# Up-projection of a decoder trunk: seven half-size products per pair in place of eight, and the output projection in column halves

## The chip, the core and the metric

The kernel runs on one core of a Trainium2 chip. The metric is the device time of one execution in microseconds (us); lower is better. The core's engines work through their own instruction streams in order: TensorE (PE) for matrix products, VectorE (DVE), ScalarE (ACT), GpSimd (POOL), and SyncE (SP), whose queue issues all the transfers named here. An instruction starts when those ahead of it on its engine are through and the semaphores that it waits for have been raised.

## What is computed

One layer of a decoder: three token mixers, their gated sum `merged`, and then the part that the change touches (S = D = 1024, D_FF = 2816):

```python
x = x + merged @ w_o[l]
x = x + _conv_ffn(_rmsnorm(x, norm_ffn[l]), ffn_w_up[l], ffn_conv_w[l], ffn_conv_b[l], ffn_w_down[l])
...
def _conv_ffn(h, w_up, conv_w, conv_b, w_down):
    u = h @ w_up
    up = jnp.pad(u, ((0, 0), (CONV_WIDTH - 1, 0), (0, 0)))
    u = sum(conv_w[j] * up[:, j:j + S] for j in range(CONV_WIDTH)) + conv_b
    gate, val = jnp.split(u, 2, axis=-1)
    return (jax.nn.silu(gate) * val) @ w_down
```

## The kernel before

Every product is made in three: an operand is split into a rounded high part (`act`, on ACT) and the rest, its low part (`tt`, source minus high part, on DVE or POOL); `hilo` (L105) makes both. Then high x high, high x low and low x high are summed in one accumulation. A matmul takes 128 columns of weights and 512 of the moving operand.

Four stages matter here. `phase_a` ends with the branch products (tile `bps`) and loads and splits `w_o`. `phase_o` (L1289) takes eight blocks of 128 rows: it splits `merged` (`mh`, `ml`), multiplies by `w_o` in two column halves (`ops_`, 24 matmuls each), adds x, stores the sum to DRAM (`xD`), and calls `norm_block`: Square on ACT, the reciprocal root on POOL (`rs_r`), `y` on DVE, eight transposes on PE (`ntp`), and the split into `h2h` and `h2l`. `phase_up` makes the 2816 gate and 2816 value channels in 22 pairs of 128 + 128. For each of the two columns of a pair: 48 matmuls into a two-bank PSUM tile `ups_`, then the causal convolution of width 3 straight from PSUM (ACT `Identity` into `cv`, two `stt` on DVE); then Silu on ACT and the product with the value on POOL into `self.g`, which stays in SBUF. The weights are loaded and split a column ahead (`whi` on ACT, `wlo` on POOL). `phase_down` (L1358) multiplies g by `w_down`, 22 steps of 24 matmuls for each half of the rows; its first weights and its first g (`dn0`, `g0`) are made during `phase_up`.

No order is written out by hand: a list scheduler with its own cost table lays out every engine's stream when the program is built, and it is fixed from then on. Tile pools with a stated number of buffers decide what waits for what.

## Time and profile before

| | us |
|---|---|
| time, median of 3 runs | 2163.57 (2162.49 to 2165.92) |
| the profiled execution: time | 2172.32 |
| its span | 2170.5 |
| mean granted TensorE clock, share of full speed | 0.989 |
| first `ups_` matmul to first `dps_` matmul | 1438.06 to 1913.29 |

The span is one execution seen by the hardware profiler, 1.8 us short of that execution's own time. The profile gives the busy time of each engine, the idle time before an instruction, and what ended it. A matmul's shown length (0.39 us) overlaps the next; the distance from start to start is what one costs.

### The profile page before, as it was taken

How to read it: one execution, taken by the hardware profiler on the slowest of the kernel's cores; microseconds unless marked ns; L12 is line 12 of the kernel's file. 1: busy time of each engine (PE TensorE's matmuls, PEld its weight loads, DVE VectorE, ACT ScalarE, POOL GpSimd, SP SyncE). 2: the span in 40 equal slices, each digit the busy share in tenths (PEclk: the TensorE clock that was granted, in tenths of full speed). 3: DMA queues.
4: the chain of work that ended last, by engine and by line, in shares of the span. 5: the costliest groups of instructions: out<-in, count | busy, mean ns of one | idle time of the engine just before them, and what ended most of it. 6: DMA issues, size and time to landing. Idle time of an engine off the chain costs nothing. (4 is left out here: it accounts for less than half of the span.)

```text
span 2170.5 us, 32037 instructions
## 1 busy us (share of the span) xinstructions
PE 2098.8 (97%) x12818; PEld 1680.4 (77%) x12818; DVE 945.1 (44%) x1956; ACT 740.2 (34%) x1270; POOL 694.0 (32%) x522
## 2 busy tenths in 40 slices
PE   7999999999999998999888999999999999999998
PEld 6877777777777776777677777888888888878887
DVE  7035255243433523566677764432222222243534
ACT  5332222232232223666545442232222222232322
POOL 3152333152243323364155556013333333300000
PEclk9999999999999999999999999999999999999999
DMA  5222232122222214300375444221111111142521
GB/s 178 84 71 78 63 88 66 51 85 62 73 68 78 82 60 131 95 16 11 94 221 175 149 145 160 97 80 49 49 49 49 49 49 49 39 155 98 174 98 59
DMA packets 127447, 191.39 MB, mean 88 GB/s; under 512 B 60064, under 2 KB 64032, under 8 KB 127296
## 3 DMA queue, kind: packets, MB, share of 16 engines
...
q14 instruction: 50, 0.41, 0.1%
...
## 5 line engine op out<-in xcount | busy, mean ns | idle before, releaser
L89 POOL TENSOR_TENSOR wlo<-wraw,whi 128x512 fp32r<-128x512 f32 (+1 forms) x174 | 276.1, 1594 | 582.4 <-ACT whi L86 245.3
L65 PE MATMUL gps<-hhi,whi 128*128 128x512 f32 (+1 forms) x880 | 346.5, 397 | 8.1 <-ACT sp L86 5.4
L65 PE MATMUL gps<-hlo,whi 128*128 128x512 f32 (+1 forms) x880 | 342.6, 392 | 0.0
L86 ACT ACTIVATE whi<-wraw 128x512 fp32r<-128x512 f32 (+1 forms) x174 | 128.0, 737 | 426.4 <-DMA wraw<-in_w_rest_dram 106.3
L65 PE MATMUL gps<-hhi,wlo 128*128 128x512 f32 (+1 forms) x880 | 226.2, 394 | 2.1 <-DVE lx L99 1.7
L65 PEld LDWEIGHTS gps<-hhi,whi 128*128 128x128 f32 x880 | 168.0, 191 | 49.4 <-ACT sp L86 6.2
L65 PEld LDWEIGHTS gps<-hlo,whi 128*128 128x128 f32 x880 | 167.9, 191 | 36.0 <-issue 4.5
L65 PEld LDWEIGHTS gps<-hhi,wlo 128*128 128x128 f32 x880 | 157.4, 188 | 43.1 <-issue 6.7
L89 POOL TENSOR_TENSOR rs_r<-rs_v,phalf 128x1 f32<-128x1 f32 (+2 forms) x43 | 40.2, 935 | 391.9 <-DVE rs_v L96 383.8
L86 ACT ACTIVATE L<-L,m 128x128 f32<-128x128 f32 (+7 forms) x128 | 98.8, 772 | 69.1 <-DVE m L89 47.5
L77 PE MATMUL ptp<-ident,L 128*128 128x128 f32 x432 | 72.4, 282 | 10.7 <-DVE L L99 2.9
L89 DVE TENSOR_TENSOR gl<-g,gh 128x512 fp32r<-128x512 f32 x43 | 29.5, 692 | 108.8 <-ACT gh L86 107.6
L99 DVE SCALAR_TENSOR_TENSOR st<-pr,gam,fc 128x64 f32<-128x64 f32 x60 | 17.0, 283 | 128.0 <-PE pr L65 127.8
L86 ACT ACTIVATE gh<-g 128x512 fp32r<-128x512 f32 x43 | 26.8, 630 | 131.9 <-PE dps__19477 L65 67.2
L77 PEld LDWEIGHTS ptp<-ident,L 128*128 128x128 f32 x432 | 49.2, 142 | 26.9 <-issue 15.0
L89 POOL TENSOR_TENSOR g<-cv 128x1024 f32<-128x1024 f32 x22 | 52.6, 2390 | 51.7 <-DVE cv L99 50.2
L878 DVE CUSTOM_DVE_ANT_0 L<-S,mband,rq 128x512 f32<-128x512 f32 (+3 forms) x96 | 57.1, 612 | 19.5 <-PE ptp L77 9.7
L89 DVE TENSOR_TENSOR wdl<-wdr,wdh 128x1024 fp32r<-128x1024 f32 x44 | 53.8, 1225 | 15.9 <-ACT wdh L86 15.9
L86 ACT ACTIVATE sp<-gps,hbg 128x512 f32<-128x512 f32 x48 | 32.9, 686 | 75.1 <-PE gps L65 67.9
L65 PE MATMUL bps<-oh,whi 128*128 128x512 f32 x128 | 53.2, 421 | 5.1 <-DVE merged L99 3.2
L89 POOL TENSOR_TENSOR merged<-merged,gth 128x512 f32<-128x512 f32 x32 | 47.6, 1491 | 29.1 <-DVE gth L99 26.3
L878 DVE CUSTOM_DVE_ANT_0 L<-S,bias 128x512 f32<-128x512 f32 (+3 forms) x96 | 50.7, 551 | 12.5 <-PE ptp L77 6.1
...
## 6 DMA issues: line engine op xcount, KB each, us to landing
wraw<-in_w_up_dram SPq DMA_DIRECT2D x44, 512.0 KB, 3.3
wdr<-in_w_down_dram SPq DMA_DIRECT2D x44, 512.0 KB, 3.3
wraw<-in_w_rest_dram SPq DMA_DIRECT2D x80, 256.0 KB, 2.9
pD<-sp SPq DMA_DIRECT2D x78, 256.0 KB, 2.0
gth<-pD SPq DMA_DIRECT2D x48, 256.0 KB, 3.0
x<-in_x_dram SPq DMA_DIRECT2D x16, 512.0 KB, 5.5
wraw<-in_w_rw_dram SPq DMA_DIRECT2D x28, 256.0 KB, 3.0
draw<-pD SPq DMA_DIRECT2D x24, 256.0 KB, 5.0
```

What stands on the lines that cost most here:

```text
L65: ins = self.nc.tensor.matmul(out, lhsT, rhs, start=start, stop=stop)
L77: self.marked(self.nc.tensor.transpose(out, in_, ident))
L86: self.nc.scalar.activation(out, in_, func, **kw)
L89: (eng or self.nc.vector).tensor_tensor(out, a, b, op)
L99: self.nc.vector.scalar_tensor_tensor(out, a, s, b, op0, op1)
L878: self.nc.vector.tensor_tensor_reduce(L[:, c0:c0 + w], ps[:, :w], bias[:, c0:c0 + w], scale, 3.0e38, ALU.add, ALU.min, acc)
```

## The change

**Up-projection.** Rows 0 to 511 and 512 to 1023 of the normed input, each cut in two halves of the 1024 summed channels, and the gate and value weights, cut the same way, form a 2 x 2 by 2 x 2 product, which is made with seven half-size products (`n2`, `m4`, `m3`, `n5`, `m1`, `m6`, `m7`) in place of eight: 7 x 12 matmuls a pair in place of 96. The seven moving operands (`X`) are made once, in `operands`, while the norms run; the seven weights of a pair are made in `up_weight`, five of them from a sum or difference of two raw blocks (`wsum`, DVE), then a high part (`wh`, ACT) and a low part (`wl`, POOL; for `m6` DVE). The products come together from three banks in `after` into `C` in SBUF, and the convolution reads `C`.

**Output projection.** First all eight blocks for columns 0 to 511, then for columns 512 to 1023 in the order 0, 1, 4, 2, 5, 3, 6, 7, with norm, transposes and `operands`. The first half of `w_o` lies in a pool of its own (`woa`), whose memory takes `xm1` and `xm6`; that of `merged` takes `xm7` and raw up-weights.

**g** goes through DRAM (`gD`): stored by pair, read back in `phase_down` by `down_g`, in 44 loads; `dn0` and `g0` are gone.

```diff
+            self.W, self.woa = [], self.pool(woa, "woa", 1, "right")
+            for c, wp in enumerate((self.woa, self.pool(wob, "wob", 1, "right"))):
...
-    def phase_o(self):
+    def phase_o(self, wob, up):
...
+            seq = [(0, b) for b in range(8)] + [(1, b) for b in (0, 1, 4, 2, 5, 3, 6, 7)]
+            nxt = split(0)
+            for n, (c, b) in enumerate(seq):
+                mh, bs = nxt, slice(128 * b, 128 * b + 128)
+                if c and b == 0:
+                    for m, tag in (("m1", "woh"), ("m6", "wol")):
+                        t = self.woa.tile([128, 2, 4, 512], F32R, tag=tag, name="x" + m)
+                        self.X[m] = [t[:, 0], t[:, 1]]
                 x = xp.tile([128, D], F32, tag="x2", name="x2")
...
+                cs = slice(512 * c, 512 * c + 512)
+                if c:
+                    nc.sync.dma_start(x[:, 0:512], self.xD[b, :, 0:512])
+                nc.sync.dma_start(x[:, cs], self.i["x"][0, bs, cs])
+                ps = aps.tile([128, 512], F32, tag="o", name="ops_")
+                w = self.W[c]
+                self.mm3(ps, lambda k: (mh[0][:, k], mh[1][:, k]), lambda k: (w[0][:, k], w[1][:, k]), 8)
+                self.tt(x[:, cs], ps, x[:, cs], ALU.add)
+                if n < 15:
+                    nxt = split(seq[n + 1][1])
...
+                    self.up_open(wob, up)
+                    ts = rows()
+                    for m, k in (("n2", 0), ("m4", 4)):
+                        self.up_w[0, m] = self.up_weight(0, m, [t[:, k:k + 4] for t in ts])
+                    for m in ("n2", "m4"):
+                        self.up_begin(0, m)
+                nc.sync.dma_start(self.xD[b, :, cs], x[:, cs])
+                if not c:
+                    continue
+                y, p = self.norm_rows(x, g, o2, 1), []
+                for q in range(2):
+                    p.append(tps.tile([128, 4, 128], F32, tag="ntp", name="ntp"))
+                    for k in range(4):
+                        col = 128 * (4 * q + k)
+                        self.tr(p[q][:, k], y[:, col:col + 128], self.ident)
+                if b == 7:
+                    for j, m in ((1, "n2"), (1, "m4"), (0, "m3")):
+                        self.up_prepare(j, m)
+                self.operands(b, p, o2)
+            for m in ("n5", "m1", "m6", "m7"):
+                self.up_prepare(0, m)
...
+    def operands(self, b, p, sp):
...
+        lower, vec, pool = b < 4, self.nc.vector, self.nc.gpsimd
+        first, second, names = (p[0], p[1], ("n2", "m4")) if lower else (p[1], p[0], ("n5", "m3"))
+        bs = slice(128 * (b % 4), 128 * (b % 4) + 128)
+        T = lambda tag: sp.tile([128, 4, 128], F32, tag=tag, name=tag, bufs=1)
+        at = lambda n: [t[:, :, bs] for t in self.X[n]]
+        neg, dif, a = T("neg"), T("dif"), T("xa")
+        kept = [self.hD[b % 4, k].rearrange("p (k n) -> p k n", k=4) for k in range(3)]
+        self.act(neg, first, scale=-1.0)
+        self.tt(dif, second, neg, ALU.add)
+        self.hilo(*at(names[0]), neg)
+        self.hilo(*at(names[1]), dif, lo_eng=pool if lower else vec)
+        if lower:
+            self.act(a, second)
+            self.nc.sync.dma_start(kept[0], neg)
+            self.nc.sync.dma_start(kept[1], a)
+            return
+        c = T("xc")
+        self.nc.sync.dma_start(a, kept[0])
+        self.nc.sync.dma_start(c, kept[1])
+        self.tt(a, a, neg, ALU.add, pool)
+        h, l = at("m1")
+        self.act(h, a, scale=-1.0)
+        self.stt(l, a, -1.0, f32v(h), ALU.mult, ALU.subtract)
+        self.tt(dif, dif, a, ALU.subtract)
+        self.hilo(*at("m6"), dif, lo_eng=vec)
+        self.tt(c, c, neg, ALU.subtract, pool)
+        self.nc.sync.dma_start(kept[2], c)
...
+    def up_open(self, wob, up):
...
+        t = self.mgp.tile([128, 2, 4, 512], F32R, tag="mb", name="xm7")
+        self.X["m7"] = [t[:, 0], t[:, 1]]
+        t = self.mgp.tile([128, 3, 8, 128], F32, tag="ma", name="wraw")
+        self.raw.update({(1, 1): t[:, 0], (0, 0): t[:, 1], (1, 0): t[:, 2]})
+        for j, e in ((1, 1), (0, 0), (1, 0)):
+            self.up_load(j, e)
+        wob.close()
...
+    def up_weight(self, j, n, w=None):
+        a = lambda e, k: self.raw[j % 2, e][:, 4 * k:4 * k + 4]
+        x, y, op = {"n2": ((1, 0), (1, 1), ALU.add), "m4": ((1, 1), None, None), "m3": ((0, 0), None, None),
+                    "n5": ((0, 0), (0, 1), ALU.add), "m1": ((0, 0), (1, 1), ALU.add),
+                    "m6": ((1, 0), (0, 0), ALU.subtract), "m7": ((0, 1), (1, 1), ALU.subtract)}[n]
+        src = a(*x)
+        if y:
+            src = self.wsum[0]
+            self.wsum = self.wsum[1:] + self.wsum[:1]
+            self.tt(src, a(*x), a(*y), op)
+        vec = w or n == "m6"
+        w = w or [self.upr.tile([128, 4, 128], F32R, tag=n + m, name="w" + m) for m in "hl"]
+        self.hilo(*w, src, lo_eng=self.nc.vector if vec else None)
+        return w
...
+    def up_begin(self, j, n):
...
+        if n == "n2":
+            for m in "bc":
+                u[m] = self.ups.tile([128, 512], F32, tag=m, name="ups_" + m)
+        if n == "m1":
+            u["a"] = self.upq.tile([128, 512], F32, tag="a", name="ups_a")
+        ps = u[{"n2": "b", "m4": "c", "m3": "b", "n5": "c", "m1": "a", "m6": "b", "m7": "c"}[n]]
+        self.up_product(ps, n, self.up_w.pop((j, n)), n in ("n2", "m4", "m1"))
+        return ps
+    def up_product(self, ps, n, w, first):
+        x = self.X[n]
+        terms = [(k, a, c) for k in range(4) for a, c in ((0, 0), (0, 1))] + [(k, 1, 0) for k in range(4)]
+        for i, (k, a, c) in enumerate(terms):
+            self.mm(ps, w[a][:, k], x[c][:, k], first and i == 0, i == 11, skip_group_check=not first)
...
+            def after(j, n, ps):
+                u = self.pairs[j]
+                if n == "n2":
+                    u["C"] = [t2.tile([128, S], F32, tag="C%d" % e, name="C") for e in range(2)]
+                gate, val = u["C"]
+                if n in ("n2", "m4", "m1"):
+                    u[n] = T(n)
+                    self.act(u[n], ps)
+                if n == "m4":
+                    self.tt(val[:, lo], u["m4"], u["n2"], ALU.subtract, nc.gpsimd)
+                elif n == "m3":
+                    u["w"] = T("w")
+                    self.tt(u["w"], ps, val[:, lo], ALU.add)
+                elif n == "n5":
+                    self.stt(gate[:, hi], ps, -1.0, u["w"], ALU.mult, ALU.add)
+                elif n == "m6":
+                    self.tt(val[:, hi], ps, u["m1"], ALU.add)
+                elif n == "m7":
+                    self.tt(gate[:, lo], ps, u["m1"], ALU.add)
...
+            def conv(j, C):
...
+                for e in (1, 0):
+                    c, t = j + NFF * e, T("cv%d" % e, S)
+                    self.act(t, C[e], AF.Identity, scale=cw[:, c, 2:3], bias=cw[:, c, 3:4])
+                    for d in (1, 2):
+                        self.stt(t[:, d:], C[e][:, :S - d], cw[:, c, 2 - d:3 - d], t[:, d:], ALU.mult, ALU.add)
                     ts.append(t)
-                self.act(ts[0], ts[0], AF.Silu)
-                self.tt(self.g[:, j], ts[0], ts[1], ALU.mult, nc.gpsimd)
+                self.act(ts[1], ts[1], AF.Silu)
+                self.tt(ts[1], ts[1], ts[0], ALU.mult, nc.gpsimd)
+                nc.sync.dma_start(self.gD[j], ts[1])
...
+            start = [((1, "n2"), ""), ((1, "m4"), ""), ((0, "m3"), ""), ((0, "n5"), "1m3 1n5"), ((1, "m3"), ""),
+                     ((1, "n5"), ""), ((0, "m1"), ""), ((0, "m6"), "1m1"), ((0, "m7"), "1m6"), ((1, "m1"), "1m7 2n2"),
...
+            for j in range(2, NFF):
+                for n in self.ORDER:
+                    after(j, n, self.up_begin(j, n))
+                    self.up_prepare(last[0] + 1, last[1])
+                    last = j, n
+                    if n == "n5":
+                        loads(j + 2)
...
+    def down_g(self, pool, j, cols, bufs, tag="graw"):
+        raw = pool.tile([128, 512], F32, tag=tag, name="graw", bufs=bufs)
+        self.nc.sync.dma_start(raw, self.gD[j, :, cols])
...
-                        self.hilo(*g, self.g[:, j, tgs], lo_eng=nc.vector)
+                    w, g = self.down_w(wp, j), self.down_g(gp, j, tgs, 4)
                     ws.append((j, w, g))
```

**Where instructions stand now.** On DVE, in the middle of `phase_up` before, there was nothing but the convolution, each pair of rows reading the PSUM tile `ups_`:

```order
L99 SCALAR_TENSOR_TENSOR cv_16597<-ups__16596,cw_15988,cv_16597 128x1023
L99 SCALAR_TENSOR_TENSOR cv_16597<-ups__16596,cw_15988,cv_16597 128x1022
L99 SCALAR_TENSOR_TENSOR cv_16656<-ups__16655,cw_15988,cv_16656 128x1023
L99 SCALAR_TENSOR_TENSOR cv_16656<-ups__16655,cw_15988,cv_16656 128x1022
L99 SCALAR_TENSOR_TENSOR cv_16717<-ups__16716,cw_15988,cv_16717 128x1023
```

On DVE after, one whole pair (`w` and `C` with `ups_` are sums out of PSUM, `wsum` a sum of two raw weight blocks, named once where both lie in one tile, `cv1`/`cv0` the convolutions; the pair's other two rows, `w` and a first `C` out of PSUM, stand just ahead):

```order
L89 TENSOR_TENSOR wsum1_16122<-wraw_16113 128x512
L89 TENSOR_TENSOR wsum_15289<-wraw_15290 128x512
L89 TENSOR_TENSOR C_17705<-ups_b_17690,m1_17783 128x512
L89 TENSOR_TENSOR wl_17834<-wsum0_16121,wh_17833 128x512
L89 TENSOR_TENSOR wsum0_16121<-wraw_16113 128x512
L99 SCALAR_TENSOR_TENSOR cv1_17821<-C_17705,cw_16244,cv1_17821 128x1023
L89 TENSOR_TENSOR C_17704<-ups_c_17691,m1_17783 128x512
L99 SCALAR_TENSOR_TENSOR cv1_17821<-C_17705,cw_16244,cv1_17821 128x1022
L89 TENSOR_TENSOR wsum1_16122<-wraw_16113,wraw_15290 128x512
L89 TENSOR_TENSOR wsum_15289<-wraw_15290,wraw_16113 128x512
L99 SCALAR_TENSOR_TENSOR cv0_17825<-C_17704,cw_16244,cv0_17825 128x1023
L99 SCALAR_TENSOR_TENSOR cv0_17825<-C_17704,cw_16244,cv0_17825 128x1022
```

On POOL after, the same pair, from one `C` to the next (before, a pair was two `wlo` 128x1024 and one product `g`):

```order
L89 TENSOR_TENSOR C_17705<-m4_17725,n2_17706 128x512
L89 TENSOR_TENSOR cv0_17678<-cv0_17678,cv1_17674 128x1024
L89 TENSOR_TENSOR wl_17765<-wraw_16113,wh_17764 128x512
L89 TENSOR_TENSOR wl_17787<-wsum1_16122,wh_17786 128x512
L89 TENSOR_TENSOR wl_17805<-wsum_15289,wh_17804 128x512
L89 TENSOR_TENSOR wl_17857<-wsum1_16122,wh_17856 128x512
L89 TENSOR_TENSOR wl_17877<-wsum_15289,wh_17876 128x512
L89 TENSOR_TENSOR wl_17895<-wraw_15290,wh_17894 128x512
L89 TENSOR_TENSOR C_17852<-m4_17872,n2_17853 128x512
```

What moved: the convolution reads `C` in SBUF, six more instructions with both inputs in SBUF stand between its parts, and POOL has eight instructions a pair where it had three.

At the end of the output projection, on PE before, 24 matmuls of the first up-projection column stood ahead of the last block's transposes (their end is shown), and more of that column behind them:

```order
L65 MATMUL ups__15996<-h2h_15271,whi_15961 128x512
L65 MATMUL ups__15996<-h2l_15272,whi_15961 128x512
L65 MATMUL ups__15996<-h2h_15271,wlo_15962 128x512 x8
L77 MATMUL ntp_15943<-ident_93,y_15936 128x128 x4
L77 MATMUL ntp_15950<-ident_93,y_15936 128x128 x4
L65 MATMUL ups__15996<-h2h_15271,whi_15961 128x512
L65 MATMUL ups__15996<-h2l_15272,whi_15961 128x512
```

On PE after, around the sixth block's transposes (row block 3, `ntp_15987`), and then on ACT between the fifth block's `neg` and that block's `neg` (`y_15980` is the sixth block's Square):

```order
L77 MATMUL ntp_15913<-ident_95,y_15906 128x128 x4
L77 MATMUL ntp_15918<-ident_95,y_15906 128x128 x4
L65 MATMUL ops__16086<-woh1_14930,ml_16039 128x512 x3
L77 MATMUL ntp_15987<-ident_95,y_15980 128x128 x4
L77 MATMUL ntp_15992<-ident_95,y_15980 128x128 x4
L65 MATMUL ups_b_16130<-xn2h_15278,mh_16123 128x512
L65 MATMUL ups_b_16259<-xn2h_15278,wh_16176 128x512
```

```order
L86 ACTIVATE neg_15923<-ntp_15918 128x512
L86 ACTIVATE y_15980,ss_15979<-x2_15943 128x1024
L86 ACTIVATE wh_16180<-wraw_16113 128x512
L86 ACTIVATE xn5h_15284<-neg_15923 128x4x128
L86 ACTIVATE wh_16184<-wraw_16113 128x512
L86 ACTIVATE wh_16214<-wsum_15289 128x512
L86 ACTIVATE wh_16176<-wsum0_16121 128x512
L86 ACTIVATE xm1_15595<-xa_15925 128x4x128
L86 ACTIVATE xm3h_15282<-dif_15924 128x4x128
L86 ACTIVATE wh_16209<-wsum1_16122 128x512
L86 ACTIVATE neg_15997<-ntp_15987 128x512
```

What moved: three matmuls stand between the two sets of transposes, and the first up-projection matmul stands right behind; on ACT eight splits stand between the Square and the next `neg`.

On SP before, at the end of `phase_up`, the final norm's gain and the second to fourth down-weights (the first stands 43 rows earlier):

```order
L1366 DMA gf_18654<-in_norm_final_dram 128x1024
L1354 DMA wdr_18688<-in_w_down_dram 128x1024
L1354 DMA wdr_18722<-in_w_down_dram 128x1024
L1354 DMA wdr_18756<-in_w_down_dram 128x1024
L1378 DMA x3_19330<-xD_60 128x1024
```

On SP after, at the same place:

```order
L1536 DMA graw_19642<-gD_62 128x512
L1536 DMA graw_19678<-gD_62 128x512
L1536 DMA graw_19714<-gD_62 128x512
L1489 DMA gD_62<-cv0_19415 128x1024
L1548 DMA gf_19446<-in_norm_final_dram 128x1024
L1529 DMA wdr_19456<-in_w_down_dram 128x1024
L1529 DMA wdr_19492<-in_w_down_dram 128x1024
```

What moved: `gf` and the first down-weight `wdr` now stand behind the store of the last pair's g, and that store waits for POOL's last product.

## Rows read from the trace of the kernel before

**Rows 1.** The page: busy time of each engine, share of the span, instructions.

```profile
PE 2098.8 (97%) x12818; PEld 1680.4 (77%) x12818; DVE 945.1 (44%) x1956; ACT 740.2 (34%) x1270; POOL 694.0 (32%) x522
```

**Rows 2.** Windows: us, busy (count) by engine, granted clock, DMA share, GB/s.

```profile
1420.00:1438.00 18.00, 18.00 (x88) 14.97 (x87) 6.08 (x9) 3.33 (x6) 0.55 (x1) 1.00 0.14 56
1750.00:1850.00 100.00, 100.00 (x443) 82.84 (x442) 23.08 (x18) 25.73 (x23) 32.42 (x14) 1.00 0.14 48
2030.00:2130.00 100.00, 100.00 (x439) 82.12 (x439) 45.11 (x59) 33.64 (x52) 2.19 (x4) 1.00 0.41 137
```

**Rows 3.** Timeline of POOL, DVE and ACT in the up-projection, one pair: start, us, engine.

```profile
1701.43 2.41 POOL L89 TENSOR_TENSOR wlo<-wraw,whi 128x1024 fp32r<-128x1024 f32 x1 [8.47 <-ACT whi L86]
...
1716.22 1.06 ACT L86 ACTIVATE cv<-cv 128x1024 f32<-128x1024 f32 x1 [2.80 <-DVE cv L99]
...
1723.19 2.41 POOL L89 TENSOR_TENSOR wlo<-wraw,whi 128x1024 fp32r<-128x1024 f32 x1 [8.48 <-ACT whi L86]
1724.34 2.60 DVE L99 SCALAR_TENSOR_TENSOR cv<-ups__17495,cw,cv 128x1023 f32<-128x1023 f32 x2 [8.21 <-ACT cv L86]
1727.08 2.39 POOL L89 TENSOR_TENSOR g<-cv 128x1024 f32<-128x1024 f32 x1 [1.48 <-DVE cv L99]
```

**Rows 4.** The page's groups: busy, mean ns of one, idle before and releaser.

```profile
L89 DVE TENSOR_TENSOR gl<-g,gh 128x512 fp32r<-128x512 f32 x43 | 29.5, 692 | 108.8 <-ACT gh L86 107.6
L86 ACT ACTIVATE gh<-g 128x512 fp32r<-128x512 f32 x43 | 26.8, 630 | 131.9 <-PE dps__19477 L65 67.2
L89 POOL TENSOR_TENSOR g<-cv 128x1024 f32<-128x1024 f32 x22 | 52.6, 2390 | 51.7 <-DVE cv L99 50.2
```

**Rows 5.** Timeline of DVE and POOL at the end of `phase_a`.

```profile
1307.59 3.51 POOL L89 TENSOR_TENSOR merged<-merged,gth 128x512 f32<-128x512 f32 x2
1308.64 3.54 DVE L89 TENSOR_TENSOR wol<-woraw,woh 128x1024 fp32r<-128x1024 f32 x2 [2.48 <-ACT woh L86]
...
1323.33 1.22 DVE L89 TENSOR_TENSOR wol<-woraw,woh 128x1024 fp32r<-128x1024 f32 x1
1323.49 2.21 POOL L89 TENSOR_TENSOR merged<-merged,gth 128x512 f32<-128x512 f32 x1 [1.49 <-DVE gth L99]
...
1329.28 1.29 POOL L89 TENSOR_TENSOR merged<-merged,gth 128x512 f32<-128x512 f32 x1
```

**Rows 6.** Groups by form, 1343 to 1438 (output projection).

```profile
L99 DVE SCALAR_TENSOR_TENSOR y<-x,rs_r,gain 128x1024 f32<-128x1024 f32 x7 | 9.0, 1285 | 5.0 <-POOL rs_r L89 5.0
L86 ACT ACTIVATE h2h<-ntp 128x512 fp32r<-128x512 f32 x14 | 7.6, 596 | 50.5 <-PE ntp L77 50.5
L86 ACT ACTIVATE y<-x 128x1024 f32<-128x1024 f32 x7 | 7.4, 1062 | 10.5 <-issue 8.0 <-DVE x L89 2.5
L89 POOL TENSOR_TENSOR rs_r<-rs_v,phalf 128x1 f32<-128x1 f32 x7 | 3.9, 551 | 74.7 <-DVE rs_v L96 74.7
```

**Rows 7.** What PE waited for, 1300 to 2170: us in total, times, longest.

```profile
PE dps__18661 L65 <- DVE cv L99: 1.8, 1, 1.8
...
PE ups__15996 L65 <- ACT h2h L86: 0.2, 1, 0.2
PE ups__15996 L65 <- DVE h2l L89: 0.2, 1, 0.2
```

**Rows 8.** Timeline of PE where the up-projection ends.

```profile
1924.22 0.47 PE L65 MATMUL dps__18661<-wdh,g 128*128 128x512 f32 x1 [1.84 <-DVE cv L99]
...
1925.31 0.63 PE L65 MATMUL dps__18662<-wdh,g 128*128 128x512 f32 x1
1925.73 0.63 PE L65 MATMUL dps__18662<-wdl,g 128*128 128x512 f32 x1
```

**Rows 9.** Windows there (columns as in the second group).

```profile
1926.00:1928.00 2.00, 2.00 (x6) 1.54 (x6) 1.42 (x2) 2.00 (x4) 0.59 (x1) 0.50 0.98 344
1928.00:1930.00 2.00, 2.00 (x10) 1.64 (x9) 2.00 (x4) 1.90 (x4) 0.00 (x0) 1.00 1.00 387
```

**Rows 10.** Transfers: count, KB each, median us from issue to landing.

```profile
wdr<-in_w_down_dram SPq DMA_DIRECT2D x44, 512.0 KB, 3.3
...
gth<-pD SPq DMA_DIRECT2D x48, 256.0 KB, 3.0
...
xD<-x SPq DMA_DIRECT2D x8, 512.0 KB, 2.6
```

More of the change, by code (lines that the diff above doesn't have):

```diff
@@ L193, in norm_block, with norm_rows @@
             self.tt(lo[:, gs, bs], p, f32v(hi[:, gs, bs]), ALU.subtract)
+    def norm_rows(self, x, gain, sp, ybufs, eps=1e-6):
+        ss = sp.tile([128, 1], F32, tag="ss", name="ss")
+        y = sp.tile([128, D], F32, tag="y", name="y", bufs=ybufs)
+        self.act(y, x, AF.Square, accum_out=ss)
+        r = self.rstd(sp, ss, 1, 1.0 / D, eps, "nt")
+        self.stt(y, x, r, gain, ALU.mult, ALU.mult)
+        return y
     def gain(self, pool, src):
@@ L1291, in phase_o, with rows, split @@
             aps, tps = P("ops2", 2, space=PSUM), P("tps2", 2, space=PSUM)
-            W = self.W
             g = self.gain(xp, self.i["norm_ffn"])
-            for b in range(8):
-                bs = slice(128 * b, 128 * b + 128)
-                mh = [o2.tile([128, 8, 128], F32R, tag="m" + n, name="m" + n) for n in "hl"]
+            def rows():
+                return [o2.tile([128, 8, 128], F32R, tag="m" + n, name="m" + n) for n in "hl"]
+            def split(b):
+                mh, bs = rows(), slice(128 * b, 128 * b + 128)
                 for ks, m in zip((slice(0, 3), slice(3, 8)), self.merged):
@@ new lines @@
+    ORDER = ("n2", "m4", "m3", "n5", "m1", "m6", "m7")
+    def up_open(self, wob, up):
[6 more added lines that the diff above has]
+        wob.close()
+        self.upr = self.pool(up, "upr", 1, "right")
+        self.wsum += [self.upr.tile([128, 4, 128], F32, name="wsum%d" % k) for k in range(2)]
@@ new lines, in up_prepare @@
+    def up_prepare(self, j, n):
+        if j < NFF:
+            self.up_w[j, n] = self.up_weight(j, n)
+    def up_begin(self, j, n):
+        u = self.pairs.setdefault(j, {})
+        if n == "n2":
[6 more added lines that the diff above has]
+        return ps
@@ L1314, in phase_up @@
             P = lambda *a, **k: self.pool(es, *a, **k)
-            wps = [self.upw, P("wp3", 1)]
-            t2 = P("u2", 2)
-            cw = P("cw", 1).tile([128, 44, 4], F32, name="cw")
+            t1, t2 = P("u1", 1), P("u2", 2)
+            self.upq = P("upq", 1, space=PSUM)
+            cw = t1.tile([128, 44, 4], F32, name="cw")
             nc.sync.dma_start(cw, self.i["conv"])
-            order = [j + NFF * e for j in range(NFF) for e in range(2)]
-            def weights(n):
-                if n < 2 * NFF:
-                    self.wp = wps[n % 2]
-                    return self.load_w(self.i["w_up"][order[n]], 8, 128, bufs=(1, 1), raws=1)
@@ new lines, in loads @@
+            def loads(j):
+                for e in (1, 0):
+                    self.up_load(j, e)
+            kept = []
+            for q in range(4):
+                if q % 2 == 0:
+                    t = T("cv%d" % (q // 2), S).rearrange("p (a k n) -> p a k n", a=2, k=4)
+                kept.append(t[:, q % 2])
+                nc.sync.dma_start(kept[q], self.hD[q, 2].rearrange("p (k n) -> p k n", k=4))
+            for n, m in (("n2", "b"), ("m4", "c")):
+                after(0, n, self.pairs[0][m])
@@ new lines, in phase_up @@
+            start = [((1, "n2"), ""), ((1, "m4"), ""), ((0, "m3"), ""), ((0, "n5"), "1m3 1n5"), ((1, "m3"), ""),
+                     ((1, "n5"), ""), ((0, "m1"), ""), ((0, "m6"), "1m1"), ((0, "m7"), "1m6"), ((1, "m1"), "1m7 2n2"),
+                     ((1, "m6"), "2m4 2m3"), ((1, "m7"), "2n5 2m1 2m6")]
+            for i, (jn, todo) in enumerate(start):
+                after(*jn, self.up_begin(*jn))
+                for t in todo.split():
+                    self.up_prepare(int(t[0]), t[1:])
+                if i < 4:
+                    bs = slice(128 * i, 128 * i + 128)
+                    self.hilo(*[t[:, :, bs] for t in self.X["m7"]], kept[i], lo_eng=(nc.vector, nc.gpsimd)[i % 2])
+                if jn == (0, "m1"):
+                    loads(2)
+                if jn == (1, "m7"):
+                    loads(3)
```

104 lines of the change are left out of this document (37 added, 67 removed).

## Prediction

> **What bounds the kernel now.** I read the page first: PE is busy for 97% of the span and no other engine for half of it [rows 1]. The windows say where that holds. Through the up-projection PE is busy for 100 of 100 us at the full granted clock, with DVE at 23, ACT at 26 and POOL at 32 of the 100, DMA at a share of 0.14; in the down-projection PE is full too, with DMA at 0.41 [rows 2]. The list of waits shows what is left: 0.4 us where the up-projection begins and 1.8 us where it ends [rows 7]. So PE's own work sets the time, and fewer matmuls give their time back as long as the other engines keep up. A pair of columns takes 21.76 us (from one low part of its weights to that of the next pair, 1701.43 to 1723.19) [rows 3], 0.2267 us for each of its 96 matmuls.
>
> **What the change takes away.** 12 matmuls for each of 22 pairs: 12 x 0.2267 = 2.72, so 22 x 2.72 = 59.8 us. A pair on PE alone becomes 84 x 0.2267 = 19.04 us.
>
> **What the change adds to a pair elsewhere.** DVE: four sums out of PSUM, five weight sums and the low part of m6, ten of 128x512 at 0.69 [rows 4], and four convolution steps of 128x1023 at 1.28 (two ran 2.60) [rows 3]: 12.0 us. POOL: seven instructions of 128x512 (six low parts and one `C`) at 1.29 [rows 5] and the product at 2.39 [rows 4]: 11.4 us. ACT: seven high parts at 0.63 [rows 4], three copies out of PSUM at 0.60 [rows 6], two Identity and a Silu at 1.06 [rows 3]: 9.4 us. Each is below 19.04, and by these sums PE stays the bound.
>
> **But DVE and POOL don't run side by side.** At 1307.59 two POOL additions (1.29 each alone) and two DVE subtractions (1.22 each alone), all of whose inputs lie in SBUF, overlap. The first pair shows 3.51 us instead of 2.58, the second 3.54 instead of 2.44, and both together last from 1307.59 to 1312.18: 4.59 us, where one after another without overlap would be 5.02. At 1323.49 a single POOL addition that meets a DVE subtraction takes 2.21: it waits for its end at 1324.55 and then needs 1.15 [rows 5]. Where the DVE instruction reads PSUM, nothing of the kind shows: the convolution's two steps run at 1.30 each over a POOL low part of 2.41, the length of both without company [rows 3]. The up-projection of before has only that harmless sort on DVE. After the change the convolution reads `C` from SBUF, and the weight sums and m6's low part read SBUF twice.
>
> The Trainium skill (SBUF — State Buffer, section "Who interferes with whom") has the same as a rule: a DVE instruction with two SBUF inputs contends with a GpSimd instruction that reads SBUF, and whichever comes second waits for the whole of the first. Taken to the letter it would make the instructions below cost their full 20.7 us in line; the trace shows 4.59 for 5.02, so I go on with the smaller figure.
>
> Per pair, what has to take turns (a turn is the time for which one keeps the other out): DVE 4 x 1.28 + 6 x 0.69 = 9.26 and POOL 7 x 1.29 + 2.39 = 11.42, together 20.68, by the measured ratio 4.59/5.02 = 0.914 some 18.9 us. That alone is PE's 19.04. And the turns can't follow each other without gaps, because both engines work in order. Following the two streams through a pair: behind the second convolution step of `cv0` comes the Silu on ACT (1.06 and two handovers of about 0.1), and POOL can't pass the product that waits for it, while DVE has only sums out of PSUM there: 1.3 us in which nobody takes a turn. At the pair's beginning, between the last weight sum (which waits for POOL's low part of m1, since the three `wsum` buffers are all in use) and m6's low part, DVE sums m6 out of PSUM (0.69) and then waits for a high part on ACT (about 0.6): 1.2 us more. So a pair takes DVE, POOL and ACT about 18.9 + 2.5 = 21.4 us, almost what it took before. Bounds: 19.04, if other work fills every gap, and 20.7 + 2.5 = 23.2, if every turn lasts as long as the instruction. I take 21.4, since I find nothing in the two streams that could fill the gaps, and the ratio is measured.
>
> PE then loses 21.4 - 19.04 = 2.36 us per pair. Where: m6 can't start before `w` is out of m3's bank, and `w` stands on DVE behind all four convolution steps; in the first such pair it is there 3 us early, which one pair's delay uses up. The first two pairs' weights are made apart, the last pair makes none, and one goes for those 3 us: 18 pairs, +42.5 us.
>
> **Where the up-projection begins.** Before: 0.4 us [rows 7], with 24 matmuls in front of the last transposes. Now the norm, the operands and the first weights of two pairs are made in the same stretch, in order. Take the sixth block. When the fifth block's transposes end, ACT does `neg` (0.60) [rows 6], the sixth's Square (1.06) [rows 6], five high parts and that of m1 (6 x 0.63) [rows 4]; DVE stands before m1's low part (0.69), and only then makes `y` (1.28) [rows 6]: 7.5 us with handovers, of which PE has three matmuls to fill 0.7. So PE waits 6.8 us there; without the six high parts and the low part ahead of it, it would be 2.3. By the same chains the fifth block waits 2.1, the first product 1.9 for `neg` and its two high parts (0.60 + 2 x 0.63) and 2 more for a low part that stands behind five others on POOL, the last block 1.5, the first m1 3.1 (POOL's `xa` 1.29, a high part, a low part, handovers). Together 17.4. After a wait of 1.84 us the granted clock went to 0.50 and nine matmuls started 0.43 apart rather than 0.227 [rows 8, 9]: 1.8 us. Three such waits here, 5.4: 22.8 us, less the 0.4 of before: +22.4. Bounds: 9, if the scheduler's order costs only the shortest chain at each block, and 30, since low parts on POOL and DVE take turns here as well.
>
> **Where it ends.** Before, PE waited 1.8 us for the last convolution and lost 1.8 to the clock. Now the first down-weight can't be issued before the last pair's g is stored and the norm's gain is loaded into the memory that this frees. From the end of the last m7: sum out of PSUM 0.7, Identity 1.06 (behind the value's), two convolution steps, Silu 1.06, product 2.39: 9.7 us. Then the store (2.6 for as many bytes, xD) [rows 10], the load of w_down (3.3) [rows 10], its high part (1.06, as the Silu's) [rows 3], and handovers and issues of 0.7: 17.3 us, in which PE has nothing, and 2.9 for the clock (14 matmuls at half rate; after 1.84 it was nine). Less 3.6: +16.6. Bounds 14 and 19, by how the transfers land.
>
> **What costs nothing.** The column halves have the same 384 matmuls and 64 transposes; half of x is read twice, at a DMA share of 0.14 [rows 2]. g adds 11.5 MB written over 410 us and 11.5 MB read over some 240, 48 GB/s to the 137 at a share of 0.41 [rows 2], four buffers deep (11 us of PE work) against a landing of 3 us [rows 10]; without that cover it would cost its landing time once.
>
> **Sum.** -59.8 + 42.5 + 22.4 + 16.6 = +21.7. The profiled execution took 2172.3, 1.8 over its span and 8.7 over the median of 2163.57; by the same difference the median becomes 2185.
>
> **Rivals.**
> *The turns don't bind* (0.26). DVE and POOL slip into each other's gaps, a pair takes PE's 19.04: -59.8 + 22.4 + 16.6 = -20.8, 2143. For it: each engine alone has 7 us a pair to spare, and weights are made up to 18 us ahead. Against it: [rows 5]. It decides from 1.2 us a pair (20.8/18): above that the change loses, below it wins.
> *Half of it* (0.10): turns cost 1.0 to 1.4 a pair, and all ends within 0.2% of before, which is about what a measurement of this kernel can tell from no change: 2159 to 2168.
> *The ends are covered* (0.07): the start costs its lower bound of 9 and the first down-weight comes early (about 3), with the turns as forecast: -59.8 + 42.5 + 9 + 3 = -5, 2158.
> *Every turn is as long as the instruction* (0.06): 23.2 a pair, +75 in place of 42.5: 2217.
> The forecast has the rest, 0.51, for itself between 2172 and 2205. So faster 0.33, same 0.10, slower 0.57. The range 2141 to 2207 leaves out the last rival and about half of the first.
>
> **What would show it.** The distance between two POOL products in mid up-projection: 21.4 if the turns bind, 19.04 if not. PE's waits there: on DVE `w`, once a pair, 2.4 us. Convolution steps longer than 1.28 and POOL's low parts longer than 1.29 where they overlap. At the start a wait of nearly 7 us for the sixth block's `y`; at the end one of 17 us for the first high part of w_down, with gD's last store ahead of it on SP. I am wrong if the convolution from SBUF runs at 1.3 over POOL's work, or if the scheduler's gaps happen to fit.

## The result, and the profile after

The changed kernel takes 2214.96 us, median of 4 runs (2212.35 to 2218.94), beside 2164.19 for the kernel before: ratio 1.0236, 95% interval 1.0216 to 1.0256. It is slower, as forecast, but by 50.8 us and not by 21, and 2215 lies outside the range. The profiled execution took 2212.9 with a span of 2211.1, 40.6 us over that of before; its mean granted clock is 0.978 (0.989).

The page of after has its engines and the three groups that the change made or lengthened (busy, mean ns of one, idle time before and its releaser):

```profile
PE 2064.7 (93%) x12554; PEld 1633.2 (74%) x12554; DVE 1214.8 (55%) x2202; ACT 832.5 (38%) x1485; POOL 873.6 (40%) x652
...
L89 DVE TENSOR_TENSOR wsum<-wraw 128x512 f32<-128x512 f32 x110 | 132.2, 1224 | 93.0 <-POOL wl L89 91.8
L89 POOL TENSOR_TENSOR wl<-wsum,wh 128x512 fp32r<-128x512 f32 x87 | 146.2, 1698 | 84.1 <-ACT wh L86 74.3
...
L99 DVE SCALAR_TENSOR_TENSOR cv<-C,cw,cv 128x1023 f32<-128x1023 f32 x88 | 147.5, 1678 | 5.4 <-ACT cv L86 4.3
```

PE has exactly the 264 matmuls less, and yet it is busy for 93% instead of 97% [rows 1]. The other rows say whose time that became: a weight sum takes 1.22 where an instruction of that size on DVE took 0.69 alone [rows 4], a low part on POOL 1.70 where 1.29 stood alone [rows 5], a convolution step 1.68 where the sum used 1.28. The windows of after (busy and count of PE, PEld, DVE, ACT, POOL; granted clock, DMA share, GB/s) place it:

```profile
1440.00:1460.00 20.00, 7.25 (x22) 4.95 (x21) 17.33 (x17) 10.66 (x20) 18.11 (x13) 0.59 0.32 102
...
1700.00:1800.00 100.00, 93.30 (x393) 72.34 (x392) 72.92 (x65) 40.70 (x61) 64.62 (x39) 1.00 0.21 79
1980.00:2080.00 100.00, 100.00 (x442) 82.79 (x442) 39.71 (x48) 30.53 (x44) 1.10 (x2) 1.00 0.45 147
```

In the up-projection PE starts 393 matmuls in 100 us, where before had 443 [rows 2]; in the down-projection nothing changed. Where the up-projection begins, DVE and POOL are nearly full, PE works for 7.25 of 20 us, and the clock falls. What PE waited for in after (us in total, times, longest):

```profile
PE dps__19448 L65 <- ACT wdh L86: 23.9, 1, 23.9
PE ups_b L65 <- DVE w L89: 23.1, 18, 2.7
PE ntp L77 <- DVE y L99: 11.7, 2, 8.2
...
PE ups_c L65 <- ACT m L86: 4.7, 13, 0.8
PE ops__16086 L65 <- DVE x L89: 4.1, 1, 4.1
PE ups_a L65 <- ACT xm L86: 2.8, 1, 2.8
PE ups_b L65 <- ACT xn2h L86: 2.5, 1, 2.5
PE ups_b L65 <- POOL xn2l L89: 2.1, 1, 2.1
PE ups_a L65 <- DVE xm L99: 2.0, 1, 2.0
```

Against [rows 7], all three places of the forecast are there: the pairs (`w`), the start (`ntp`, `ops_` and the first operands) and the end (`wdh`). One pair in the timeline of after, POOL, DVE and PE from answers of their own:

```profile
1742.04 2.41 POOL L89 TENSOR_TENSOR cv<-cv,cv 128x1024 f32<-128x1024 f32 x1 [3.69 <-issue]
...
1752.31 4.29 POOL L89 TENSOR_TENSOR wl<-wsum,wh 128x512 fp32r<-128x512 f32 x2 [4.13 <-ACT wh L86]
1756.56 1.73 POOL L89 TENSOR_TENSOR wl<-wraw,wh 128x512 fp32r<-128x512 f32 x1
1758.26 1.74 POOL L89 TENSOR_TENSOR C<-m,n 128x512 f32<-128x512 f32 x1
1763.68 2.40 POOL L89 TENSOR_TENSOR cv<-cv,cv 128x1024 f32<-128x1024 f32 x1 [3.68 <-issue]
...
1753.74 1.72 DVE L99 SCALAR_TENSOR_TENSOR cv<-C,cw,cv 128x1022 f32<-128x1022 f32 x1
1755.38 3.46 DVE L89 TENSOR_TENSOR wsum<-wraw 128x512 f32<-128x512 f32 x2
1758.77 3.63 DVE L99 SCALAR_TENSOR_TENSOR cv<-C,cw,cv 128x1023 f32<-128x1023 f32 x2
1762.32 0.68 DVE L89 TENSOR_TENSOR w<-ups_b,C 128x512 f32<-128x512 f32 x1
...
1763.06 2.11 PE L65 MATMUL ups_b<-xm,wh 128*128 128x512 f32 x8 [1.27 <-DVE w L89]
```

The products `cv<-cv,cv` stand 21.64 apart (1742.04 to 1763.68); the forecast was 21.4. Between 1752 and 1760 POOL and DVE stretch each other: two weight sums last 3.46 instead of 1.38, two low parts 4.29 instead of 2.58. And `w` comes behind the fourth convolution step, with m6 (the eight matmuls of `ups_b<-xm,wh`) right behind it.

### The profile page after: what moved, and what is told of

Same layout as the page of the kernel before. It is cut to its first block, busy times and chain, and to the rows that moved or that the text cites. A ratio compares the mean times of both kernels' runs of the same rounds, so it can differ in the third digit from the quotient of the medians.

```text
span 2211.1 us, 32640 instructions
## 1 busy us (share of the span) xinstructions
PE 2064.7 (93%) x12554; PEld 1633.2 (74%) x12554; DVE 1214.8 (55%) x2202; ACT 832.5 (38%) x1485; POOL 873.6 (40%) x652
## 5 line engine op out<-in xcount | busy, mean ns | idle before, releaser
L89 POOL TENSOR_TENSOR wlo<-wraw,whi 128x512 fp32r<-128x512 f32 x130 | 171.0, 1324 | 301.5 <-PE gps L65 155.1
L89 DVE TENSOR_TENSOR wsum<-wraw 128x512 f32<-128x512 f32 x110 | 132.2, 1224 | 93.0 <-POOL wl L89 91.8
L89 POOL TENSOR_TENSOR wl<-wsum,wh 128x512 fp32r<-128x512 f32 x87 | 146.2, 1698 | 84.1 <-ACT wh L86 74.3
L86 ACT ACTIVATE whi<-wraw 128x512 fp32r<-128x512 f32 x130 | 81.3, 628 | 191.8 <-DMA wraw<-in_w_rest_dram 106.5
L99 DVE SCALAR_TENSOR_TENSOR cv<-C,cw,cv 128x1023 f32<-128x1023 f32 x88 | 147.5, 1678 | 5.4 <-ACT cv L86 4.3
L86 ACT ACTIVATE wh<-wsum 128x512 fp32r<-128x512 f32 x109 | 66.2, 622 | 103.6 <-DVE wsum L89 86.9
L89 DVE TENSOR_TENSOR gl<-graw,gh 128x512 fp32r<-128x512 f32 x44 | 30.4, 692 | 120.8 <-ACT gh L86 120.8
L89 POOL TENSOR_TENSOR cv<-cv,cv 128x1024 f32<-128x1024 f32 x22 | 52.8, 2399 | 73.3 <-issue 48.9
L86 ACT ACTIVATE cv<-C,cw 128x1024 f32<-128x1024 f32 x44 | 54.6, 1241 | 70.0 <-DVE C L89 69.1
L89 POOL TENSOR_TENSOR wl<-wraw,wh 128x512 fp32r<-128x512 f32 x43 | 69.2, 1608 | 12.2 <-ACT wh L86 4.5
```

Of the source, the lines that this page charges most:

```text
L86: self.nc.scalar.activation(out, in_, func, **kw)
L89: (eng or self.nc.vector).tensor_tensor(out, a, b, op)
L99: self.nc.vector.scalar_tensor_tensor(out, a, s, b, op0, op1)
```

## The experiments

Ten kernels ran. Boundaries that I compare below are read from each timeline of PE: first `ops_`, first m3 (`xm3h`), start of the last m7's four matmuls with the low weight part ("to the last m7"), first and last `dps_`.

### Are the turns at SBUF the pair's length?

**x1_taps_psum.** The four convolution steps read their shifted input from a constant PSUM tile instead of `C`, which leaves their two terms out of the result. For that tile to fit, the down-projection's PSUM pool (`dpa`) is opened behind the up-projection and not ahead of it.

```diff
+            z = P("zz", 1, space=PSUM).tile([128, S], F32, name="zz")
+            nc.vector.memset(z, 0.0)
...
-                        self.stt(t[:, d:], C[e][:, :S - d], cw[:, c, 2 - d:3 - d], t[:, d:], ALU.mult, ALU.add)
+                        self.stt(t[:, d:], z[:, :S - d], cw[:, c, 2 - d:3 - d], t[:, d:], ALU.mult, ALU.add)
```

> The changed kernel, but the four convolution steps of a pair read their shifted input from a constant PSUM tile in place of C (so the taps are left out of the result). Same instructions, same engines, same lengths and streams; only the second SBUF input is gone. If DVE and POOL take turns at SBUF (theory A), these steps run at 1.28 over POOL's work, the distance between two POOL products falls from 21.64 to 19.0 to 19.6, PE's wait on w goes, and the time falls by 35 to 45 to about 2170 to 2180. If the pair is long because the streams wait for one another in order whatever they read (rival B), the distance stays at 21.6 and the time within 5 us of 2215.

**x3_lows_dve.** All work stays, but from the third pair on DVE makes the low parts, and POOL has one sum and the product left.

```diff
-        vec = w or n == "m6"
+        vec = w or n == "m6" or j >= 2
```

> The changed kernel with all low parts of the weights from the third pair on made on DVE (0.69 each) in place of POOL (1.29). Theory A: turns fall to DVE 9.26 + 6 x 0.69 = 13.4 and POOL 1.29 + 2.39 = 3.7, and DVE, with 16.1 us of its own, fits below PE's 19.04: distance 19.0 to 19.8, time 30 to 45 us lower, 2170 to 2185. Rival B: DVE is the longest ring of the pair already and gets 4.1 us more: distance 21.6 or longer, time 2215 or more.

x1 takes 2167.75 (ratio to before 1.0005, 0.9994 to 1.0017), x3 2168.99 (1.0011, 1.0002 to 1.0021): 47 and 46 us less than after. In x1 the convolution steps and POOL's low parts of 1500 to 1900 are back at their lengths alone, although POOL has all its work beside DVE's (the weight sums, which still read SBUF twice, are at 0.93). The products stand 19.1 to 19.7 apart, 19.40 at the median:

```profile
L99 DVE SCALAR_TENSOR_TENSOR cv<-zz,cw,cv 128x1023 f32<-128x1023 f32 x87 | 111.0, 1278 | 4.1 <-ACT cv L86 2.3
...
L89 POOL TENSOR_TENSOR wl<-wsum,wh 128x512 fp32r<-128x512 f32 x80 | 103.5, 1310 | 118.2 <-PE ups_c L65 85.0 <-ACT wh L86 29.4 <-PE ups_b L65 3.0
```

In x3 the products stand 19.42 apart, with more of the work on DVE than in after:

```profile
1715.57 2.40 POOL L89 TENSOR_TENSOR cv<-cv,cv 128x1024 f32<-128x1024 f32 x1 [2.36 <-issue]
1734.99 2.40 POOL L89 TENSOR_TENSOR cv<-cv,cv 128x1024 f32<-128x1024 f32 x1 [2.37 <-issue]
```

The rival that DVE's list alone is too long would have made x3 worse; it made it as fast as x1, which took nothing off DVE's list or POOL's. So it is the turns that two engines take, and the wait on `w` is gone in both. From the first m3 to the last m7 after needs 451.9, x1 412.6, x3 412.3. Another 4.4 us come back at the end in both, at which neither edit is aimed: PE's wait at the first `dps_` is 18.6 in x1 and 20.0 in x3, for 23.9 in after.

### The end

**x4_down_early.** The last g is stored from POOL's queue, and the norm's gain is loaded behind the fourth down-weight.

```diff
-                nc.sync.dma_start(self.gD[j], ts[1])
+                (nc.gpsimd if j == NFF - 1 else nc.sync).dma_start(self.gD[j], ts[1])
...
-            nc.sync.dma_start(gf, self.i["norm_final"].unsqueeze(0).to_broadcast([128, D]))
...
+                    if tg == 0 and j == 3:
+                        nc.sync.dma_start(gf, self.i["norm_final"].unsqueeze(0).to_broadcast([128, D]))
```

> The changed kernel with the last pair's g stored from POOL's queue and the norm's gain loaded after the fourth down-weight, so that SP can load the first four down-weights before the last product is done. Theory A for the end (the store ahead of the load on SP makes the wait): the load drops out of the chain, what stays is the first high part behind the last Silu on ACT, some 10 us after the last product and 1.1 of its own: the wait of 23.9 becomes 11 to 12.5 and the time falls by 11 to 13, to about 2203. Rival: the transfers themselves are late (DMA full at that place), then the wait stays above 18.

2203.24 (1.0167, 1.015 to 1.0184), 11.7 less than after. The wait at the first `dps_` went from 23.9 to 13.0, where 11 to 12.5 was expected:

```profile
PE dps__19447 L65 <- ACT wdh L86: 13.0, 1, 13.0
```

In the timeline of after (SP, then POOL, ACT and PE) the chain that this cut is plain:

```profile
1952.37 0.32 SPq L1489 DMA_DIRECT2D gD<-cv  x1
1954.99 0.33 SPq L1548 DMA_DIRECT2D gf<-in_norm_final_dram  x1
1955.37 1.94 SPq L1529 DMA_DIRECT2D wdr<-in_w_down_dram  x4
...
1950.01 2.34 POOL L89 TENSOR_TENSOR cv<-cv,cv 128x1024 f32<-128x1024 f32 x1 [15.24 <-ACT cv L86]
...
1960.69 1.06 ACT L86 ACTIVATE wdh<-wdr 128x1024 fp32r<-128x1024 f32 x1 [10.81 <-DMA wdr<-in_w_down_dram]
...
1961.80 0.80 PE L65 MATMUL dps__19448<-wdh,gh 128*128 128x512 f32 x1 [23.91 <-ACT wdh L86]
```

The store waits for the product, the gain for the store's landing, and the down-weights stand behind both on SP.

### The start

**s1_start_dve.** All low parts and sums of the operands, and the low parts of the first two pairs' weights, go to DVE.

```diff
-        self.hilo(*at(names[0]), neg)
-        self.hilo(*at(names[1]), dif, lo_eng=pool if lower else vec)
+        self.hilo(*at(names[0]), neg, lo_eng=vec)
+        self.hilo(*at(names[1]), dif, lo_eng=vec)
...
-        self.tt(a, a, neg, ALU.add, pool)
+        self.tt(a, a, neg, ALU.add)
...
-        self.tt(c, c, neg, ALU.subtract, pool)
+        self.tt(c, c, neg, ALU.subtract)
...
-        vec = w or n == "m6"
+        vec = w or n == "m6" or j < 2
```

> The changed kernel with every low part and sum of the operands, and the low parts of the first two pairs' weights, on DVE in place of POOL. Theory A for the start (turns stretch what the chains are made of): y runs at 1.28 in place of 2.28 and rs_r at 0.55, PE's waits between 1425 and 1485 fall from 25 to about 17 and the time by 8 to 12. Rival (queues alone): DVE gets 23 x 0.69 = 16 us more in a stretch of 75 in which it is busy for 53, its queue ahead of each y gets longer, and the waits stay at 25 or grow.

2204.27 (1.0171, 1.0155 to 1.0188), 10.7 less than after. The sixth block's `y` in s1, and before it that of after, each from a timeline of DVE:

```profile
1445.70 1.29 DVE L99 SCALAR_TENSOR_TENSOR y<-x,rs_r,gain 128x1024 f32<-128x1024 f32 x1 [0.44 <-POOL rs_r L89]
```

```profile
1446.22 2.28 DVE L99 SCALAR_TENSOR_TENSOR y<-x,rs_r,gain 128x1024 f32<-128x1024 f32 x1 [0.44 <-POOL rs_r L89]
```

The same instruction is 1 us shorter without POOL's low parts beside it. It starts half a microsecond sooner, but so does the whole stage in s1 (its first `ops_` at 1340.54, after's at 1341.07): counted from there it starts no sooner, and the transposes still wait 7.5 for it. From first `ops_` to first m3 after needs 143.9, s1 137.6, and 2.0 more come back between first m3 and last m7. So about a fifth of the 33 us that the start costs (below) were turns there. PE's waits at the start fall from 25.1 to 19.0 in all (17 was expected); those that are left (7.5 for `y`, 6.0 for m1's high part, 3.3 for `x`, 1.7 and 0.5) stay in a kernel in which the operands' low parts are all made on DVE. That the order of the streams makes these is read from the timelines, and no run changed that order.

### All together

**c1_all.** s1, x4, and `vec = True` (the low parts of all weights on DVE).

> The three edits together: all low parts and the operands' sums on DVE throughout, the last g stored from POOL's queue, the gain loaded later. If the three losses are separate, their gains add: 46 + 12 + 11 = 69, so 2215 becomes 2146, 0.9% below the kernel before. If they were the same loss told twice (a shorter start only moves the wait to the pairs), it ends above 2157.

2152.01 (2146.89 to 2153.82) beside 2166.58: ratio 0.9927, 0.9911 to 0.9942. It beats both kernels, the one before by 0.7%, and is 63 us under after, where 69 was expected. The 69 added three differences of medians; by the spans of the profiled executions the three single gains are 44.3, 8.1 and 8.2, 60.6 in all, and c1's is 63.8. So the miss of 6 is no sign that the losses overlap. A wait of 9.0 for the first high part of w_down stays.

**c2_all_pool.** c1, with the first down-weight's two parts on POOL, the last product on DVE and its store from ACT's queue.

```diff
-                self.tt(ts[1], ts[1], ts[0], ALU.mult, nc.gpsimd)
-                nc.sync.dma_start(self.gD[j], ts[1])
+                self.tt(ts[1], ts[1], ts[0], ALU.mult, None if j == NFF - 1 else nc.gpsimd)
+                (nc.scalar if j == NFF - 1 else nc.sync).dma_start(self.gD[j], ts[1])
...
+        if eng:
+            eng.tensor_copy(w[0], raw)
+            self.tt(w[1], raw, f32v(w[0]), ALU.subtract, eng)
```

> As the kernel with the three edits, and at the end the first down-weight's two parts are made on POOL, the last product on DVE, its store issued from ACT's queue. If the rest of the wait at the end (13) is the first high part standing behind the last Silu on ACT, PE starts the down-projection within 2 us, works 5.4 us on the first weight and then waits some 5 for the second: 6 us in place of 13, 2139. If something else holds the first product (banks of PSUM, the transfer), the time stays within 2 us of the kernel with three edits.

2151.03 (0.9928, 0.9914 to 0.9942): no gain over c1, a miss. The timelines of SP and POOL in c2 say why:

```profile
1881.20 0.32 SPq L1489 DMA_DIRECT2D gD<-cv  x1
1881.62 10.16 SPq L1540 DMA_DIRECT2D graw<-gD  x8
1891.83 1.37 SPq L1529 DMA_DIRECT2D wdr<-in_w_down_dram  x3
...
1896.32 2.12 POOL L1532 CAST wdh<-wdr 128x1024 fp32r<-128x1024 f32 x1 [15.15 <-DMA wdr<-in_w_down_dram]
```

Eight loads of g stand ahead of the down-weight on SP and take 10.16 to issue, since there are four buffers and the fifth waits until the first is split. The load lands 4.5 behind its issue, and POOL needs 2.12 for the high part that takes ACT 1.06. In c1 the load came no sooner than ACT was free for it (issue at 1892.51, high part at 1896.87). By these lines the kernel is late now with its own queue as much as with the engine that makes the high part; no run changed the order on that queue.

**b0_before.** The kernel before, profiled once more.

> The kernel before once more, for a second profiled execution of it: the one that the terms were made against took 2172.3, 8 us above the median. If that was that execution's own, this one lies at 2162 to 2168, and the difference sits in one stretch of its trace.

2171.04, against a median of 2166.58 for nine runs of the same kernel on that chip. 2162 to 2168 was expected. Both profiled executions of before lie above its median, by 8.7 and 4.5, but so does one of the nine others (2171.7), and the profiled one of after lies 2 below its own median. Whether a profiled execution of before is longer as a rule, and why, was not found.

### Why the matmuls of the up-projection stand wider

Even where nothing waits, c1 starts 435 matmuls in 100 us, and before had 443 [rows 2]. In c1's timeline those of n2, m4, m3 and n5 start 0.2333 apart, those of m1, m6 and m7 0.226 to 0.230. The first four have their operands in pool `h2`; the program's memory layout puts these 32 bytes past a multiple of 128, the weights 96 past one, and the operands of m1, m6 and m7 96 too. In the kernel before, operands and weights both lay at 32: pool `h2` begins at the same byte in both kernels, and it is the weights that moved. Three variants of c1 test that.

**d1_swap_x** exchanges which operands the products read, from the third pair on, so that its result is not the layer's:

```diff
+        swap = dict(zip(("n2", "m4", "m3", "m1", "m6", "m7"), ("m1", "m6", "m7", "n2", "m4", "m3")))
-        x = self.X[n]
+        x = self.X[swap.get(n, n) if j >= 2 else n]
```

> Like c1_all, but from the third pair on n2, m4 and m3 read the operands of m1, m6 and m7, and these read those of n2, m4 and m3 (so the result isn't the layer's; the work is the same). In c1_all the matmuls of n2, m4, m3 and n5 start 0.2333 us apart, those of m6 and m7 0.2263 to 0.2288. If the place of the operand in memory sets it, the wide spacing moves with the operands: m1, m6 and m7 at 0.2333, n2, m4 and m3 at 0.227 to 0.229, n5 still at 0.2333. If the product's place in the pair sets it (its bank, or the work beside it), n2, m4 and m3 keep 0.2333. The time stays within 3 us of the 2152 of c1_all in both.

**d2_pad64_x** puts 64 unused bytes ahead of the four operands:

```diff
             hp = self.pool(e4, "h2", 1)
+            hp.tile([128, 16], F32, name="pad")
```

> Like c1_all, with 64 unused bytes ahead of the operands of n2, m4, m3 and n5, which then begin at the same place in a line of 128 bytes as the weights (96 of 128; before at 32). If the wide spacing comes from that difference, all products start their matmuls 0.227 apart, 442 of them in 100 us instead of 435, and the time is 7 us below that of c1_all, 2145. If it comes from the part of memory in which the operands lie (their addresses stay below 84 KB, the weights above 131 KB), 435 and 2152 stay.

**d3_pad64_w** moves the weights from 96 to 32 instead:

```diff
             t1, t2 = P("u1", 1), P("u2", 2)
+            self.upr.tile([128, 16], F32, name="pad")
```

> Like c1_all, with 64 bytes that move the weights of the up-projection from 96 to 32 of 128, so that they agree with the operands of n2, m4, m3 and n5 and differ from those of m1, m6 and m7. If the difference counts, the wide spacing changes over: n2, m4, m3 and n5 at 0.227, m1, m6 and m7 at 0.2333, three products in place of four, and the time falls by 1.7 us to 2150, which a comparison can hardly tell; the spacing in the trace tells it. If the part of memory counts, nothing changes.

Groups by form of c1, d1 and d2 in 1600 to 1850 (the mean ns is a modelled length, but it follows the spacing: 394 with 0.2333, 389 with 0.2267):

```profile
L65 PE MATMUL ups_c<-xm,wh 128*128 128x512 f32 x99 | 24.6, 389 | 0.0
L65 PE MATMUL ups_b<-xn2h,wh 128*128 128x512 f32 x52 | 20.5, 394 | 0.0
```

```profile
L65 PE MATMUL ups_b<-xm,wh 128*128 128x512 f32 x208 | 51.9, 391 | 0.0
...
L65 PE MATMUL ups_a<-xn2h,wh 128*128 128x512 f32 x52 | 20.5, 394 | 0.0
```

```profile
L65 PE MATMUL ups_c<-xm,wh 128*128 128x512 f32 x105 | 26.1, 389 | 0.0
...
L65 PE MATMUL ups_b<-xn2h,wh 128*128 128x512 f32 x52 | 20.2, 389 | 0.0
```

In d1 the wide spacing went with the operand (m1 on `ups_a` reads `xn2h` now: 394), not with the product. In d2 it is gone everywhere, and two of POOL's products stand 19.03 apart, the forecast's 84 x 0.2267 = 19.04, where c1 has 19.40:

```profile
1706.51 2.40 POOL L89 TENSOR_TENSOR cv<-cv,cv 128x1024 f32<-128x1024 f32 x1 [4.17 <-issue]
1725.54 2.40 POOL L89 TENSOR_TENSOR cv<-cv,cv 128x1024 f32<-128x1024 f32 x1 [4.16 <-issue]
```

The windows of c1, d2 and d3:

```profile
1650.00:1750.00 100.00, 100.00 (x435) 81.10 (x434) 84.19 (x104) 48.94 (x67) 22.65 (x11) 1.00 0.23 82
```

```profile
1650.00:1750.00 100.00, 100.00 (x443) 82.83 (x442) 86.72 (x105) 48.71 (x68) 23.41 (x11) 1.00 0.23 85
```

```profile
1650.00:1750.00 100.00, 100.00 (x438) 81.94 (x437) 84.73 (x104) 49.02 (x67) 21.39 (x11) 1.00 0.24 86
```

d2 takes 2145.73 (2145.12 to 2148.11) beside 2168.58: 0.9901, 0.9882 to 0.992, the lowest median here, and 6.3 under c1, where 7 was expected. The two intervals overlap, so the gain rests on the trace: from first m3 to last m7 d2 needs 404.4, c1 412.05, 7.6 us less. d3 is less clean and not what was expected: n5 came down to 0.2267, but n2, m4 and m3 stand at 0.227 to 0.231, m1, m6 and m7 at 0.229 to 0.233, and its 2147.30 can't be told from either. d1 took 2158.0 in its one run, outside the 3 us expected; its wait at the first `dps_` was 14.9 and not 9.0: the down-weights stand behind loads of g that took 13.36 to issue there, and 9.99 in c1.

That the place of operands and weights in memory changes the spacing is shown, and that 64 bytes cure it. Which rule does it is not. It is not the operand's place alone: before had its operands at the same 32 and 0.2267. And it is not just agreement with a product's own weights: in c1 m1 and m6, both at 96 like their weights, start up to 0.230 apart, and 0.2267 in d2, where neither moved; in d3 n2, m4 and m3 agree with their weights at 32, and only n5 is back at 0.2267 throughout.

## Why the prediction was right in sign and wrong in size

By spans, which is how the forecast's sum was made:

| term | forecast | measured | measured by |
|---|---|---|---|
| 264 matmuls less | -59.8 | -59.8 | the page's count; priced at 0.2267 |
| turns of DVE and POOL in the pairs | +42.5 | +39.9 | first m3 to last m7, after less c1 (451.9 - 412.05) |
| start of the up-projection | +22.4 | +33.1 | what is left of first `ops_` to end of the last m7 |
| wider spacing of the matmuls | 0 | +7.6 | first m3 to last m7, c1 less d2 (412.05 - 404.4) |
| end | +16.6 | +20.7 | end of the last m7 to the last `dps_`, plus before's 12 `dps_` matmuls ahead of that end |
| ahead of `ops_`, and behind the last `dps_` | 0 | -0.9 | -1.8 and +0.9 |
| sum | +21.7 | +40.6 | |

The start, which is only what is left over in this table, can be counted apart: PE's waits there add up to 25.1, and 40 matmuls at the granted clock of 0.50 took 8.2 more than at 1.00, less the 0.4 of before: 32.9.

**The turns: right in mechanism, place and size.** 21.64 a pair for 21.4, the wait on `w` in 18 pairs as counted. It is not the whole of a pair's loss, as the forecast had it: 23.1 over 18 is 1.3 each, and a second, shorter wait on `m` (4.7 in all) and slower first matmuls behind a wait (8 in 2.11) hold more. From start to start a wait also costs more than the idle time that is shown, since a matmul's shown length overlaps the next. x1 and x3 remove it by two ways that share only the contention. The Trainium skill (SBUF — State Buffer, section "Who interferes with whom") gives the rule behind it; x1's PSUM side and x3's single engine agree with it, and its letter, 23.2 a pair with the forecast's gaps, is more than the 21.64 of the trace. The addition that waited in [rows 5] needed 1.15 behind the other's end and not 1.29, which would make up a part of that.

**The start: the step that failed by most.** "By the same chains" summed lengths that the rows show for instructions alone: 1.28 for `y` [rows 6], 1.29 for a POOL low part. But the contention that the same prediction had priced in the pairs holds here as well: seven of the eight `y` of after take about 2.30 each. The sixth block waited 8.2 and not 6.8, the last 3.5 and not 1.5, the first m1 4.7 and not 3.1, and a product of the output projection that waited 4.1 for `x` was not in the list at all, while the fifth block, forecast at 2.1, didn't wait: 25.1 in all for 17.4. The bound of 30 named these turns, and then the forecast didn't use it. The rest is clock: 40 matmuls at 0.50 and not 27 (three times nine), 8.2 us for 5.4. Without the turns, in s1, the waits add up to 19.0, close to the 17.4, but that is partly luck: the 3.3 for `x` was not in the list, the first m1 waits 6.0 and not 3.1, the first product 2.2 and not 3.9, and neither the fifth nor the last block waits.

**The spacing: a term that was missing.** "A pair on PE alone becomes 84 x 0.2267" took the spacing of before for granted. The weights moved in memory against the operands, and 48 of the 84 matmuls then started 0.2333 apart: 48 x 0.0066 x 22 = 7.0, and 7.6 in the trace. Nothing in the trace of before could show that.

**The end: right in mechanism, 6.6 too short in its wait.** The product started 12.1 behind the last m7, not 7.3: DVE and ACT had the first splits of g ahead of the last sums, and these waited for their transfers (the last gate half is summed at 1943.73). These loads stand on SP behind the store of the last pair but one, which after issues 3.1 before the end of the last m7, x3 7.0 and x1 8.4 before it; so the 4.4 that x1 and x3 win at the end fit as a further effect of the turns, which the forecast counted only in the pairs. The terms that the forecast lists up to the product's end also add up to 8.8 with the value's Identity, not 9.7. And the down-weight took 5.3 from issue to its high part instead of 3.3, beside the gain, three more down-weights and x; the DMA share was 0.89 in 1956 to 1961. Part of that came back: the forecast's 14 matmuls at half rate stand in no row, and the trace of after has nine, 1.9 us for 2.9.

**From sum to median.** "By the same difference the median becomes 2185" carried 8.7 us by which the profiled execution of before exceeds its other runs. After shows no such excess, so 50.8 by medians are 40.6 by spans, and about 10 us of the miss of 29 are this step. The other 19 are the terms of the table.

Of the rivals, "the turns don't bind" and its half are refuted by the distance of the products, "the ends are covered" by the waits. "Every turn is as long as the instruction" came nearest in its time, 2217, for the wrong reason.
